# Four of eight row-tile pairs by seven products in the gate and up projections of a hybrid layer

## The chip, the cores and the metric

The kernel runs on one core of one Trainium2 chip. The metric is the device time of one execution in microseconds (us). Before the change it is 1145.84 us, the median of three runs (1144.41 to 1147.18).

## The reference

One decoder layer for 256 tokens of width 2048, all in float32: a low-rank attention with 8 heads beside a state-space mixer, an output projection with a residual, a gated feed-forward part, and a gated embedding at the end. The change touches the feed-forward part, whose hidden width is 5632:

```python
x = x + mixed @ w_o[i]
hf = rms_norm(x, g_ffn_norm[i])
x = x + (jax.nn.silu(hf @ w_gate[i]) * (hf @ w_up[i])) @ w_down[i]
gate = jax.nn.sigmoid(rms_norm(x, g_ple_norm[i]) @ w_ple_gate[i])
x = x + gate * (p[i] @ w_ple_proj[i])
```

## The kernel before

**Products.** Every large matmul keeps float32 accuracy by splitting each operand into a rounded part and a remainder, hi and lo. One product of a 128 x 128 piece of activations with a 128 x 512 piece of weights is then three matmuls: hi*hi, hi*lo, lo*hi (`products`, all recorded under line L359).

**Weights.** They come in chunks of 256 rows by 512 columns (512 KB, tile `w_raw`, five buffers, loaded by the SyncE queue SP at L169). ScalarE (ACT) rounds a chunk into `w_hi` (L195), VectorE (DVE) subtracts to get `w_lo` (L196); of each there are three buffers. `split_to` and `load_to` run ahead of the matmuls by these buffers.

**Gate and up.** Eleven blocks of 512 hidden columns. In each, eight pairs j = 0..7: the gate chunk and the up chunk of the same 256 rows. Each pair has two row tiles k, two halves t of the tokens, and two matrices: a 2 x 2 by 2 x 2 matrix product of pieces, eight products. For the pairs in `MIXED` (2, 4, 6; in the first block 4, 6) a scheme with seven products is used. It needs sums of weight pieces, made by `mix`: four additions (`w_sum`, L210), the hi of the up chunk's last piece and of the two sum tiles on ACT (L213), and the lo of the same on DVE (L214, `w_last` and `w_mix`). It also needs sums of the activations (`sum`, made once by `norm_task`). There is one set of `w_last`, `w_sum` and `w_mix`, so the sums of the next mixed pair can only be written when PE has read those of the last.

**End of a block.** The gate and up sums stand in four PSUM banks (`acc`), shared products of the mixed pairs in four others (`pp_p`). `shared` combines the latter after the last mixed pair; then for each half t: DVE adds `acc` to `wsg`, ACT applies Silu, DVE subtracts `uc` from `acc`, DVE multiplies (all L343). The next block's matmuls need those `acc` banks. `gate_task` transposes `wsg` into `g` (PE, `pp_g`).

**Order.** The code is written in a plain order, and a scheduler sets each engine's order from it by priorities: `split_to` and `mix` stand 70 places ahead (`W_AHEAD`), `AHEAD` lists other tasks. Each engine runs its own list strictly in that order, and SP does too.

**Memory.** 39 slots of 4 KB per partition (`Slots`) hold all larger tiles. The residual rows `xs` (four slots) are made before the gate and up stage, lie through it, and are next used after the first block of the down projection.

Of the kernel before, what the change touches and what calls it, by code (L numbers as in the profile page):

```python
# [81 lines left out]


W_AHEAD = 70

AHEAD = {'s5_params': -50, 'x_stats': 50, 'glu_out': -25, 'gate_task': -25, 'norm_task': -100, 'latent_norms': -50, 'z_task': -200, 'head_norms': -200}

# [54 lines left out]
class Weights:  # L142
# [4 lines left out]
    def __init__(self, tc, pool, sched):  # L147
        self.tc, nc = tc, tc.nc
        self.nc, self.pool, self.sched, self.chunks = nc, pool, sched, []
        self.raw, self.part, self.n_dma, self.n_split = {}, {}, 0, 0  # L150
        self.extra, self.native = {}, set()
        self.mixed, self.kept, self.sums = set(), {}, None

    def block(self, w, k0, nk, c0, n):
        ids = []
# [9 lines left out]
    def load_to(self, i):  # L165
        while self.n_dma <= min(i, len(self.chunks) - 1):
            w, k, c0, n = self.chunks[self.n_dma]
            t = self.pool.tile([128, 2, n], F32, tag="raw", bufs=self.RAW, name="w_raw")
            self.nc.sync.dma_start(  # L169
                out=t, in_=w[k * 128:(k + 2) * 128, c0:c0 + n].rearrange("(k p) n -> p k n", p=128)  # L170
            )
            self.raw[self.n_dma] = t
            self.n_dma += 1
            for out, in_ in self.extra.pop(self.n_dma, ()):
                self.nc.sync.dma_start(out=out, in_=in_)

    def split_to(self, i):
        while self.n_split <= min(i, len(self.chunks) - 1):
# [14 lines left out]
            lo = self.pool.tile([128, 2, n], F32R, tag="w_lo", bufs=self.PART, name="w_lo")  # L193
            with self.tc.high_priority(W_AHEAD):
                self.nc.scalar.activation(out=hi, in_=raw, func=AF.Copy)  # L195
# [7 lines left out]
    def mix(self, g, u):  # L203


        V, A, s = self.nc.vector, self.nc.scalar, self.sched
        last, raws, parts = self.sums

        def add(o, a, b):
            V.tensor_tensor(out=o, in0=a, in1=b, op=ALU.add)  # L210

        def part(h, l, r):
            A.activation(out=h, in_=r, func=AF.Copy)  # L213
            V.tensor_tensor(out=l, in0=r, in1=h.bitcast(F32), op=ALU.subtract)  # L214

        with self.tc.high_priority(W_AHEAD):
            add(raws[0][:, 0], g[:, 0], u[:, 0])
            add(raws[0][:, 1], u[:, 0], u[:, 1])
            part(last[:, 0], last[:, 1], u[:, 1])
            add(raws[1][:, 0], raws[0][:, 0], u[:, 1])  # L220
            add(raws[1][:, 1], raws[1][:, 0], g[:, 1])
            for r, (h, l) in zip(raws, parts):
                part(h, l, r)
        s.act += 5 * 512 * 0.83e-3 + 3 * 0.19
        s.dve = max(s.dve + 9 * 512 * 1.05e-3 + 0.42, s.act)
        (h0, l0), (h1, l1) = parts
        return ((last[:, 0], last[:, 1]), (h0[:, 0], l0[:, 0]), (h0[:, 1], l0[:, 1]),
                (h1[:, 0], l1[:, 0]), (h1[:, 1], l1[:, 1])), None, s.dve

    def take(self, i):  # L230
        self.split_to(i + self.PART - 1)
        self.load_to(i + self.PART - 1 + self.RAW)
        hi, lo, t = self.part.pop(i)
        self.sched.pe = max(self.sched.pe, t)
        return hi, lo
# [3 lines left out]
def hybrid_layer_kernel(  # L239
# [6 lines left out]
    nc = tc.nc  # L246
# [7 lines left out]
    dram = ctx.enter_context(tc.tile_pool(name="scratch", bufs=1, space=bass.MemoryType.DRAM))  # L254

    S = Slots(big, [f"s{i}" for i in range(39)])
    PP = Slots(psb, [f"pp{i}" for i in range(4)])
    sched = Sched(tc)
    W = Weights(tc, wts, sched)

    blk = {}
# [13 lines left out]
    blk["glu"] = [W.block(w_glu, 0, 8, 512 * b, 512) for b in range(2)]  # L275
    blk["wos"] = [W.block(w_o, 8, 8, 512 * b, 512) for b in range(4)]
    blk["gu"] = []
    MIXED = (2, 4, 6)
    for b in range(11):
        ids = []  # L280
        for j in range(8):
# [8 lines left out]
    def wait_get(shape, name, dtype=F32):  # L290
        n = 0
        while True:
            t = S.try_get(shape, name, dtype)
            if t is not None:
                return t
            sched.step()
            sched.pe += 1.0
            n += 1
            if n > 2000:
                raise RuntimeError(f"no slot for {name}: {S.held()}")  # L300

    def wait_n(n, shape, name, dtype=F32):
        return [wait_get(shape, name, dtype) for _ in range(n)]
# [18 lines left out]
    r_a, r_s, r_f, r_p = (stat(n, 2) for n in ("r_a", "r_s", "r_f", "r_p"))  # L322
# [19 lines left out]
    def tt(o, a, b, op=ALU.mult):  # L342
        V.tensor_tensor(out=o, in0=a, in1=b, op=op)  # L343
        sched.dve += size(o) * 1.05e-3 + 0.1
# [9 lines left out]
    def act(o, i, f, **k):  # L354
        A.activation(out=o, in_=i, func=f, **k)  # L355
        sched.act += size(o) * 0.83e-3 + 0.19 + 0.09 * sum(n in k for n in ("accum_out",))
# [86 lines left out]
    NWU = 30  # L443
    X0, B0, NE = 18, 8, 22
    GATE = "y0"


    def s5_params():
# [778 lines left out]
    acc = block(blk["zq"], lhs_h, need_h)  # L1227
# [3 lines left out]
    acc = block(blk["zkv"], lhs_h)  # L1231
# [6 lines left out]
    acc = block(blk["u"][0], lhs_h)  # L1238
# [3 lines left out]
    acc = block(blk["u"][1], lhs_h)  # L1242
# [26 lines left out]
    xs = [wait_n(2, [128, 1024], "xs") for _ in range(2)]  # L1269
# [13 lines left out]
    for p, (lo, hi) in enumerate(blk["woa"]):  # L1283
        acc = accs2(), accs2()
# [74 lines left out]
    fh = wait_n(4, [128, 4, 256], "fh", F32R)  # L1359
    fl = wait_n(4, [128, 4, 256], "fl", F32R)  # L1360
    rows = {j: wait_get([128, 2, 512], "sum", F32R) for j in MIXED}
    lhs_s = tiles4(sh, sl, 8)
# [4 lines left out]
    for b in range(4):  # L1367
        acc = block(blk["wos"][b], lhs_s, need_s)
# [6 lines left out]
    lhs_f = tiles4(fh, fl)  # L1375
    wsg = wait_n(2, [128, 2, 512], "wsg")
    uc = wait_get([128, 2, 512], "uc")
    W.sums = (wait_get([128, 2, 512], "w_last", F32R), wait_n(2, [128, 2, 512], "w_sum"),
              [wait_n(2, [128, 2, 512], "w_mix", F32R) for _ in range(2)])
    gr, gh, gl = [], [], []  # L1380

    def gate_task(b):
# [92 lines left out]
    for b in range(11):  # L1475
        ws = wsg[b % 2]
        acc = mixed_block(blk["gu"][b], lhs_f, rows, ws, uc, need_f)
        if b == 0:
            total_rstd(r_f, ss_f)
        for t in range(2):  # L1480
            tt(ws[:, t], ws[:, t], acc[2 * t], ALU.add)
            act(ws[:, t], ws[:, t], AF.Silu, scale=r_f[:, t:t + 1])
            tt(uc[:, t], acc[2 * t + 1], uc[:, t], ALU.subtract)
            tt(ws[:, t], ws[:, t], uc[:, t])
        sched.add(gate_task(b), 0)
    S.put(*fh, *fl, *rows.values(), uc, W.sums[0], *W.sums[1], *W.sums[2][0], *W.sums[2][1])
    lhs_g = tiles4(gh, gl)

    def need_g(k):
# [9 lines left out]
    for b in range(4):  # L1499
        ph.append(wait_get([128, 4, 256], "ph", F32R))  # L1500
        pl.append(wait_get([128, 4, 256], "pl", F32R))
        acc = block(blk["down"][b], lhs_g, need_g)
# [119 lines left out]
```

## Time and profile before

| what | value |
|---|---|
| runs before, median | 1145.84 us |
| the profiled execution | 1146.05 us, its span 1144.1 us |
| gate and up stage in the span | 317.5 to 796.4 us |
| down stage | 796.4 to 1039.5 us |
| granted TensorE clock | 0.998 |

Rows of groups read: line, engine, operation, output<-inputs, shapes, count | busy us, mean ns of one | idle time before them and what ended it. Rows of stretches read: start:end, length, then busy us (and number of instructions) of PE, PEld (weight loads), DVE, ACT, POOL, the granted clock, the DMA share and GB/s. Rows in order of time read: start, length, what.

### The profile page before, as it was taken

What the parts mean: (1) busy time and instruction counts of PE and PEld (TensorE: products, weight loads), DVE (VectorE), ACT (ScalarE), POOL (GpSimd) and SP (SyncE); (2) the same over time, 40 slices, a digit from 0 to 9 for tenths busy, and PEclk for the clock granted to TensorE, in tenths of its full rate; (3) what the DMA queues carried; (4) which work ended last, traced back from release to release, by engine and by line L of the source; (5) the groups of instructions that cost most, each with busy time, mean ns of one, the idle gap of its engine ahead of it and who ended that gap; (6) DMA issues with size and microseconds to landing.
All of it is one profiled execution on the core that took longest, in us unless ns stands there. A gap on an engine that the chain in (4) does not pass through costs nothing.

```text
span 1144.1 us, 15655 instructions
## 1 busy us (share of the span) xinstructions
PE 1117.7 (98%) x5842; PEld 923.7 (81%) x5842; DVE 861.4 (75%) x1233; ACT 648.3 (57%) x921; POOL 19.0 (2%) x40
## 2 busy tenths in 40 slices
PE   9998999999999999999999999999999999999998
PEld 6877877889887877877877877878888888888886
DVE  7988999658698898888898898899645454546554
ACT  7863994636665555655655655557534344436443
POOL 1000020000000000000000000000000000000000
PEclk9999999999999999999999999999999999999999
DMA  9996471355566656665665665665665655555662
GB/s 336 247 259 191 117 229 33 109 190 179 183 187 200 204 184 185 204 196 180 211 192 178 210 186 178 217 183 184 202 194 186 197 188 191 188 192 187 213 209 91
DMA packets 112188, 216.97 MB, mean 190 GB/s; under 512 B 8032, under 2 KB 12912, under 8 KB 112112
## 3 DMA queue, kind: packets, MB, share of 16 engines
q1 hardware_dynamic: 109808, 211.23, 58.9%
q0 software_dynamic: 2304, 4.74, 1.5%
q8 instruction: 46, 0.75, 0.3%
q14 instruction: 30, 0.25, 0.1%
HBM read 212.66 MB, written 3.28 MB: 189 GB/s over the span
## 4 chain that ended last, share of the span: by engine, by line
PE 78%; DVE 9%; DMA 5%; ACT 4%; issue 2%; POOL 0%; DVEq 0%; SPq 0%; ACTq 0%; POOLq 0%
PE acc L359 67%; PE pp_p L359 5%; DMA w_raw<-in_w_up_dram 4%; DVE w_lo L196 3%; ACT w_hi L195 2%; DMA e<-in_bE_dram 1%; PE pp_g L386 1%; PE pp_at L359 1%; DVE w L750 1%; PE pp_at L1003 1%; PE pp_n L386 1%; PE pp_v L731 1%; DVE w_sum L210 1%; ACT L355 1%; PE pp_y L785 1%
## 5 line engine op out<-in xcount | busy, mean ns | idle before, releaser
L196 DVE TENSOR_TENSOR w_lo<-w_raw,w_hi 128x1024 fp32r<-128x1024 f32 (+2 forms) x350 | 420.8, 1206 | 207.4 <-ACT w_hi L195 206.1
L195 ACT ACTIVATE w_hi<-w_raw 128x1024 fp32r<-128x1024 f32 (+2 forms) x350 | 366.1, 1047 | 350.7 <-PE acc L359 318.9
L359 PE MATMUL acc<-w_hi,fh 128*128 128x512 f32 x480 | 188.7, 396 | 5.9 <-DVE uc L343 5.8
L359 PE MATMUL acc<-w_lo,fh 128*128 128x512 f32 x480 | 188.1, 392 | 0.0
L359 PE MATMUL acc<-w_hi,fl 128*128 128x512 f32 x480 | 187.1, 390 | 0.0
L359 PE MATMUL acc<-w_hi,gh 128*128 128x512 f32 x352 | 137.3, 390 | 0.0
L359 PE MATMUL acc<-w_hi,gl 128*128 128x512 f32 x352 | 137.1, 389 | 0.0
L359 PE MATMUL acc<-w_lo,gh 128*128 128x512 f32 x352 | 137.0, 389 | 0.0
L359 PEld LDWEIGHTS acc<-w_hi,fh 128*128 128x128 f32 x480 | 90.1, 188 | 30.9 <-DVE uc L343 12.4
L359 PEld LDWEIGHTS acc<-w_hi,fl 128*128 128x128 f32 x480 | 90.1, 188 | 18.8
L359 PEld LDWEIGHTS acc<-w_lo,fh 128*128 128x128 f32 x480 | 90.2, 188 | 17.5 <-DVE w_lo L196 0.2
L213 ACT ACTIVATE w_mix<-w_sum 128x1024 fp32r<-128x1024 f32 x64 | 67.9, 1062 | 50.3 <-DVE w_sum L210 38.5
L359 PEld LDWEIGHTS acc<-w_hi,gl 128*128 128x128 f32 x352 | 66.1, 188 | 13.8
L359 PEld LDWEIGHTS acc<-w_lo,gh 128*128 128x128 f32 x352 | 66.1, 188 | 13.6
L359 PEld LDWEIGHTS acc<-w_hi,gh 128*128 128x128 f32 x352 | 66.1, 188 | 13.6 <-DVE uc L343 0.2
L214 DVE TENSOR_TENSOR w_mix<-w_sum,w_mix 128x1024 fp32r<-128x1024 f32 x64 | 76.3, 1218 | 0.6
L359 PE MATMUL pp_p<-w_mix,sum 128*128 128x512 f32 x288 | 70.5, 389 | 0.0
L359 PEld LDWEIGHTS pp_p<-w_mix,sum 128*128 128x128 f32 x288 | 54.1, 188 | 11.2
L210 DVE TENSOR_TENSOR w_sum<-w_raw 128x512 f32<-128x512 f32 x64 | 42.2, 687 | 27.7 <-DMA w_raw<-in_w_up_dram 26.5
L359 PE MATMUL acc<-w_hi,ph 128*128 128x512 f32 x128 | 49.8, 389 | 0.0
L359 PE MATMUL acc<-w_lo,ph 128*128 128x512 f32 x128 | 49.8, 389 | 0.0
L359 PE MATMUL acc<-w_hi,pl 128*128 128x512 f32 x128 | 49.8, 389 | 0.0
(308 smaller groups left out, 1713.0 us busy)
## 6 DMA issues: line engine op xcount, KB each, us to landing
w_raw<-in_w_gate_dram SPq DMA_DIRECT2D x88, 512.0 KB, 4.2
w_raw<-in_w_up_dram SPq DMA_DIRECT2D x88, 512.0 KB, 4.6
w_raw<-in_w_down_dram SPq DMA_DIRECT2D x88, 512.0 KB, 3.7
w_raw<-in_w_o_dram SPq DMA_DIRECT2D x32, 512.0 KB, 3.7
w_raw<-in_w_ple_gate_dram SPq DMA_DIRECT2D x32, 512.0 KB, 4.1
w_raw<-in_w_in_dram SPq DMA_DIRECT2D x24, 512.0 KB, 7.6
w_raw<-in_w_glu_dram SPq DMA_DIRECT2D x8, 512.0 KB, 4.4
w_raw<-in_w_uq_dram SPq DMA_DIRECT2D x8, 384.0 KB, 3.5
```

Of the source, the lines that this page charges most:

```text
L195: self.nc.scalar.activation(out=hi, in_=raw, func=AF.Copy)
L196: self.nc.vector.tensor_tensor(out=lo, in0=raw, in1=hi.bitcast(F32), op=ALU.subtract)
L210: V.tensor_tensor(out=o, in0=a, in1=b, op=ALU.add)
L213: A.activation(out=h, in_=r, func=AF.Copy)
L214: V.tensor_tensor(out=l, in0=r, in1=h.bitcast(F32), op=ALU.subtract)
L355: A.activation(out=o, in_=i, func=f, **k)
L359: T.matmul(out=o, lhsT=a, rhs=b, start=start, stop=stop)
L386: T.transpose(out=o, in_=i, identity=ident if idt is None else idt)
L731: T.matmul(out=pv[p, r * 256 + i4 * 64:r * 256 + i4 * 64 + 64], lhsT=ee[r][p, i * 64:i * 64 + 64], rhs=um[p, i, :], start=True, stop=True, ...
L750: V.tensor_tensor_scan(out=w, data0=dc, data1=w, initial=0.0, op0=ALU.mult, op1=ALU.add)
L785: T.matmul(out=o, lhsT=a[p, i, :], rhs=f[p, i, :], start=False, stop=(r == 1), tile_position=(64 * s, 64 * s))
L1003: T.matmul(out=o, lhsT=a, rhs=b_, start=False, stop=(i == 1), skip_group_check=True)
```

## The change

Four pairs of each block are mixed, (2, 3, 5, 6), in the first block (3, 5, 6). There are two sets of `w_last` and `w_mix`, used in turn; `w_sum` stays single. Two more weight buffers (`w_more`) take the chunks whose number modulo 7 is 0 or 3, so seven chunks can lie in SBUF. The slots for this come from `xs`, whose four tiles are copied to DRAM (`x_keep`) by the POOL queue and copied back after the stage. The instructions of a block's end are written with a priority of 100 places and in another order: both additions to `wsg`, then both subtractions, then both products.

```diff
@@ class Weights
-            t = self.pool.tile([128, 2, n], F32, tag="raw", bufs=self.RAW, name="w_raw")
+            if self.more and self.n_dma % 7 in (0, 3) and self.n_dma < self.more_end:
+                self.more.rotate(1)
+                t = self.more[0]
+            else:
+                t = self.pool.tile([128, 2, n], F32, tag="raw", bufs=self.RAW, name="w_raw")
...
-        last, raws, parts = self.sums
+        last, raws, parts = self.sums[0]
+        self.sums.rotate(1)
...
     def take(self, i):
-        self.split_to(i + self.PART - 1)
-        self.load_to(i + self.PART - 1 + self.RAW)
+        n, j = 0, i
+        while n < self.PART and j < len(self.chunks):
+            n += j not in self.mixed
+            j += 1
+        if j in self.mixed:
+            j += 1
+        self.split_to(j - 1)
+        self.load_to(j - 1 + self.RAW + len(self.more))
...
-    MIXED = (2, 4, 6)
+    MIXED = (2, 3, 5, 6)
...
+    NSET = 2
...
+    w_sum = wait_n(2, [128, 2, 512], "w_sum")
+    for _ in range(NSET):
+        W.sums.append((wait_get([128, 2, 512], "w_last", F32R), w_sum,
+                       [wait_n(2, [128, 2, 512], "w_mix", F32R) for _ in range(2)]))
+    W.more_end = blk["down"][0][0]
+    W.more.extend(wait_n(2, [128, 2, 512], "w_more"))
...
-        for t in range(2):
-            tt(ws[:, t], ws[:, t], acc[2 * t], ALU.add)
-            act(ws[:, t], ws[:, t], AF.Silu, scale=r_f[:, t:t + 1])
-            tt(uc[:, t], acc[2 * t + 1], uc[:, t], ALU.subtract)
-            tt(ws[:, t], ws[:, t], uc[:, t])
+        with tc.high_priority(G_AHEAD):
+            for t in range(2):
+                tt(ws[:, t], ws[:, t], acc[2 * t], ALU.add)
+                act(ws[:, t], ws[:, t], AF.Silu, scale=r_f[:, t:t + 1])
+            for t in range(2):
+                tt(uc[:, t], acc[2 * t + 1], uc[:, t], ALU.subtract)
+            for t in range(2):
+                tt(ws[:, t], ws[:, t], uc[:, t])
         sched.add(gate_task(b), 0)
+        if b == 2:
+            keep = [dram.tile([128, 1024], F32, name="x_keep") for _ in range(4)]
+            for i in range(4):
+                nc.gpsimd.dma_start(out=keep[i], in_=xs[i // 2][i % 2])
+                S.put(xs[i // 2][i % 2])
...
+    for i in range(4):
+        xs[i // 2][i % 2] = t = wait_get([128, 1024], "xs")
+        nc.gpsimd.dma_start(out=t, in_=keep[i])
```

The first place is DVE's list at the end of a block, from the last weight work before it on. Before, in the sixth block (L196 splits, L210 weight sums, L343 the block's end):

```order
L196 TENSOR_TENSOR w_lo<-w_raw,w_hi 128x1024 x3
L343 TENSOR_TENSOR uc<-wsg,pp_p 128x512
L343 TENSOR_TENSOR wsg<-uc,pp_p 128x512
L343 TENSOR_TENSOR uc<-uc 128x512
L343 TENSOR_TENSOR wsg<-wsg,acc 128x512
L343 TENSOR_TENSOR uc<-wsg,uc 128x512
L210 TENSOR_TENSOR w_sum<-w_raw 128x512 x2
L196 TENSOR_TENSOR w_lo<-w_raw,w_hi 128x1024
L343 TENSOR_TENSOR uc<-acc,uc 128x512
L343 TENSOR_TENSOR wsg<-wsg,acc 128x512
L343 TENSOR_TENSOR wsg<-wsg,uc 128x512
L196 TENSOR_TENSOR w_lo<-w_raw,w_hi 128x1024
```

And after, at the end of the fifth block (L201, L216, L220 and L355 are the former L196, L210, L214 and L343):

```order
L220 TENSOR_TENSOR w_mix<-w_sum,w_mix 128x1024
L201 TENSOR_TENSOR w_lo<-w_more,w_hi 128x1024
L216 TENSOR_TENSOR w_sum<-w_more,w_raw 128x512
L355 TENSOR_TENSOR uc<-wsg,pp_p 128x512
L216 TENSOR_TENSOR w_sum<-w_raw 128x512
L355 TENSOR_TENSOR wsg<-uc,pp_p 128x512
L220 TENSOR_TENSOR w_last<-w_raw,w_last 128x512
L355 TENSOR_TENSOR wsg<-wsg,acc 128x512
L355 TENSOR_TENSOR uc<-uc 128x512
L216 TENSOR_TENSOR w_sum<-w_sum,w_raw 128x512
L355 TENSOR_TENSOR uc<-wsg,uc 128x512
L355 TENSOR_TENSOR uc<-acc,uc 128x512
```

The first sum of the next block's pair 2 has moved ahead of all ten instructions of the block's end; the sums of that pair that followed each other now stand between them. The four instructions that free `acc` banks, which weight work parted before, stand closer together.

The second place is the SP list with buffer numbers, around the loads for pair 2 of the same block. Before, 5092 and 5119 are gate and up of pair 2, and 5017, 5038, 5062 and 5080 the chunks of pairs 0 and 1:

```order
L169 DMA w_raw_5017<-in_w_gate_dram 128x2x512
L169 DMA w_raw_5038<-in_w_up_dram 128x2x512
L169 DMA w_raw_5062<-in_w_gate_dram 128x2x512
L169 DMA w_raw_5080<-in_w_up_dram 128x2x512
L169 DMA w_raw_5092<-in_w_gate_dram 128x2x512
L169 DMA w_raw_5119<-in_w_up_dram 128x2x512
```

After, pair 2 is w_more_3490 (gate) and 5080 (up), and 3489, 5016, 5018 and 5061 are pairs 0 and 1:

```order
L174 DMA w_more_3489<-in_w_gate_dram 128x2x512
L174 DMA w_raw_5016<-in_w_up_dram 128x2x512
L174 DMA w_raw_5018<-in_w_gate_dram 128x2x512
L174 DMA w_more_3490<-in_w_gate_dram 128x2x512
L174 DMA w_raw_5061<-in_w_up_dram 128x2x512
L174 DMA w_raw_5080<-in_w_up_dram 128x2x512
```

The order is almost that of the chunks, with some loads one place early. A load waits for the buffer of the chunk that came seven chunks earlier instead of five: the up chunk of pair 2 for the gate chunk of pair 7 of the block before, where it waited for the gate chunk of pair 0 of its own block.

The POOL list gains eight entries after the loads of `xs`: four `x_keep<-xs`, four `xs<-x_keep`, and behind them the load of `pr` that was there before.

More of the change, by code (lines that the diff above doesn't have):

```diff
@@ L84 @@
 W_AHEAD = 70
+G_AHEAD = 100
 AHEAD = {'s5_params': -50, 'x_stats': 50, 'glu_out': -25, 'gate_task': -25, 'norm_task': -100, 'latent_norms': -50, 'z_task': -200, 'head_norms': -200}
@@ L151, in __init__ @@
         self.extra, self.native = {}, set()
-        self.mixed, self.kept, self.sums = set(), {}, None
+        self.mixed, self.kept, self.sums, self.more = set(), {}, deque(), deque()
     def block(self, w, k0, nk, c0, n):
@@ L1377, in hybrid_layer_kernel @@
     uc = wait_get([128, 2, 512], "uc")
-    W.sums = (wait_get([128, 2, 512], "w_last", F32R), wait_n(2, [128, 2, 512], "w_sum"),
-              [wait_n(2, [128, 2, 512], "w_mix", F32R) for _ in range(2)])
+    w_sum = wait_n(2, [128, 2, 512], "w_sum")
[4 more added lines that the diff above has]
+    W.more.extend(wait_n(2, [128, 2, 512], "w_more"))
     gr, gh, gl = [], [], []
@@ L1479, in hybrid_layer_kernel @@
             total_rstd(r_f, ss_f)
-        for t in range(2):
-            tt(ws[:, t], ws[:, t], acc[2 * t], ALU.add)
-            act(ws[:, t], ws[:, t], AF.Silu, scale=r_f[:, t:t + 1])
-            tt(uc[:, t], acc[2 * t + 1], uc[:, t], ALU.subtract)
-            tt(ws[:, t], ws[:, t], uc[:, t])
-        sched.add(gate_task(b), 0)
-    S.put(*fh, *fl, *rows.values(), uc, W.sums[0], *W.sums[1], *W.sums[2][0], *W.sums[2][1])
+        with tc.high_priority(G_AHEAD):
[6 more added lines that the diff above has]
+                tt(ws[:, t], ws[:, t], uc[:, t])
+        sched.add(gate_task(b), 0)
+        if b == 2:
[3 more added lines that the diff above has]
+                S.put(xs[i // 2][i % 2])
+    more = list(W.more)
+    W.more.clear()
+    S.put(*more, *fh, *fl, *rows.values(), uc, *w_sum)
+    for last, _, parts in W.sums:
+        S.put(last, *parts[0], *parts[1])
+    for i in range(4):
+        xs[i // 2][i % 2] = t = wait_get([128, 1024], "xs")
+        nc.gpsimd.dma_start(out=t, in_=keep[i])
     lhs_g = tiles4(gh, gl)
```

## The prediction

> **What bounds the kernel now.** I read the page's shares first, then the chain that ended last.
>
> ```profile
> PE 1117.7 (98%) x5842; PEld 923.7 (81%) x5842; DVE 861.4 (75%) x1233; ACT 648.3 (57%) x921; POOL 19.0 (2%) x40
> PE 78%; DVE 9%; DMA 5%; ACT 4%; issue 2%; POOL 0%; DVEq 0%; SPq 0%; ACTq 0%; POOLq 0%
> ```
>
> PE is busy nearly all the time and carries 78% of the chain. DVE and DMA carry 14%, so PE is held up by them somewhere. Where, the stretches of the gate and up stage show: the whole stage, its first block, a middle block, and the last.
>
> ```profile
> 317.50:796.40 478.90, 472.22 (x2106) 385.41 (x2105) 419.57 (x507) 282.15 (x323) 0.00 (x0) 1.00 0.63 194
> 317.70:361.80 44.10, 43.99 (x199) 36.15 (x197) 38.76 (x65) 28.59 (x38) 0.00 (x0) 1.00 0.64 192
> 580.30:623.80 43.50, 42.89 (x192) 35.00 (x192) 37.69 (x45) 24.80 (x29) 0.00 (x0) 1.00 0.63 194
> 754.60:796.60 42.00, 42.00 (x188) 34.58 (x189) 40.62 (x46) 28.03 (x33) 0.00 (x0) 1.00 0.63 201
> ```
>
> A middle block takes 43.5 us; the last, with the same matmuls and no block behind it, 42.0 with PE never idle. So 1.5 us a block is lost at the boundary between blocks. DVE works 37.7 of 43.5 us: 87% here, against 75% over the kernel. The stage, and not the average, decides what four more DVE microseconds a block do. Next the chain through one boundary, merged, and PE's own rows there:
>
> ```profile
> 614.85 1.24 DVE w_lo L196
> 616.08 0.02 issue
> 616.10 4.56 DMA w_raw<-in_w_up_dram
> 620.66 0.02 issue
> 620.68 0.04 DVE w_sum L210
> ...
> 623.11 0.61 DVE uc L343
> 623.73 0.04 issue
> 623.77 2.34 PE acc L359 x9
> ```
>
> ```profile
> 621.41 0.39 PE L359 MATMUL acc<-w_hi,fl 128*128 128x512 f32 x1
> 622.77 0.39 PE L359 MATMUL acc<-w_hi,fl 128*128 128x512 f32 x1
> 623.77 0.50 PE L359 MATMUL acc<-w_hi,fh 128*128 128x512 f32 x1 [0.61 <-DVE uc L343]
> ```
>
> Between the first two rows stand six matmul intervals: (622.77 - 621.41) / 6 = 0.2267 us a matmul. Then 1.00 us passes: DVE freed the `acc` bank late, because weight sums stood ahead of that subtraction in its list and waited for a load. The load was issued when a split released its buffer, and took 4.56 us.
>
> **Seven products.** One more mixed pair saves one product, three matmuls, in each of 11 blocks: 33 x 0.2267 = 7.5 us, or 0.68 a block. All of it is on the path if PE is fed. The added pair adds no transpose.
>
> **DVE pays for it.** Here are DVE's rows of the block end, then two groups.
>
> ```profile
> 606.95 0.68 DVE L214 TENSOR_TENSOR w_last<-w_raw,w_last 128x512 fp32r<-128x512 f32 x1
> 607.55 2.35 DVE L214 TENSOR_TENSOR w_mix<-w_sum,w_mix 128x1024 fp32r<-128x1024 f32 x2
> 620.68 1.29 DVE L210 TENSOR_TENSOR w_sum<-w_raw 128x512 f32<-128x512 f32 x2 [0.53 <-DMA w_raw<-in_w_up_dram]
> 621.90 1.22 DVE L196 TENSOR_TENSOR w_lo<-w_raw,w_hi 128x1024 fp32r<-128x1024 f32 x1
> 623.03 0.68 DVE L343 TENSOR_TENSOR uc<-acc,uc 128x512 f32<-128x512 f32 x1
> 623.63 0.68 DVE L343 TENSOR_TENSOR wsg<-wsg,acc 128x512 f32<-128x512 f32 x1
> ```
>
> ```profile
> L210 DVE TENSOR_TENSOR w_sum<-w_sum,w_raw 128x512 f32<-128x512 f32 x64 | 43.8, 684 | 0.3
> L213 ACT ACTIVATE w_mix<-w_sum 128x1024 fp32r<-128x1024 f32 x64 | 67.9, 1062 | 50.3 <-DVE w_sum L210 38.5
> ```
>
> A recorded 0.68 us lets the next instruction start after 0.60 (623.03 to 623.63), a recorded 1.22 after 1.13 (621.90 to 623.03). A mixed pair adds four sums and one `w_last` at 0.60 and two `w_mix` at 1.13, and drops one `w_lo` at 1.13: 5 x 0.60 + 1.13 = 4.13 us a block. On the recorded 37.7 that makes 41.8. Counted anew by starts, twelve splits, four mixes of 5.27 and ten block-end instructions are 12 x 1.13 + 4 x 5.27 + 10 x 0.60 = 40.6. The difference is the tail of each instruction that has nothing ready behind it; the new list puts independent work between dependent pairs, so the truth lies between.
>
> PE fed would take 42.0 - 0.68 = 41.3 a block. Both engines are then full, and what DVE still waits for decides. The waits of the same block before:
>
> ```profile
> ACT w_hi L195 <- PE acc L359: 8.1, 7, 1.7
> DVE w_lo L196 <- ACT w_hi L195: 2.5, 3, 1.4
> DVE w_sum L210 <- DMA w_raw<-in_w_up_dram: 2.3, 2, 1.8
> ```
>
> The 2.5 us for ACT is back-pressure: ACT waits for PE to leave a `w_hi` buffer, so DVE was ahead. It goes when DVE has no lead. The 2.3 us for loads is not. With seven buffers one load stays late: the up chunk of pair 2, whose buffer is released by the gate split of pair 7. Between that split and the first sum of pair 2 the list holds a split, a `w_mix` and a split, 3 x 1.13 = 3.4 us, while issue and load take 0.02 + 4.56 = 4.6. DVE pauses 1.2 us, ahead of the block's end; behind it are the ten instructions that free the banks and the first up split, which PE needs after 12 matmuls (2.7 us) of the next block. By the list, all other loads have over 7 us of DVE work between release and use. So a middle block takes 40.6 + 1.2 = 41.8 to 41.8 + 1.2 = 43.0 us. I take 42.5, nearer the upper end: a split that starts after ACT has no way to hide its tail.
>
> **Boundary.** What is freed first is now in the order in which PE asks for it, and 11 instructions from the first to the last subtraction last 11 x 0.60 = 6.6 us, against 5.4 us (24 matmuls) of the last pair plus the 0.68 until the second bank is needed. The 1.5 us lost there become at most some 0.5, included in the 42.5.
>
> **ACT.** It gains two `w_mix` at 1.06 and a `w_last` of half the size, and loses one `w_hi` of the size of a `w_mix`: under 2.1 us a block on 24.8, hidden. It also runs in order: its `w_last` of pair 3 stands ahead of Silu, and would hold it until that load lands, some 3 us after the last pair begins; the multiplication that needs Silu stands over 6 us after. No cost.
>
> **First block.** 44.1 us, with DVE at 38.8 and rows of the residual in it; with 4.1 more and the pause, DVE has 44.1, and one more row sum (four additions of 0.28 us and one of 0.68) lies there or just before. I take 44.7.
>
> **Last block.** No block follows, so DVE does not bind: 41.3 + 0.3 = 41.6.
>
> ```profile
> L343 DVE TENSOR_TENSOR rows<-rows x12: 280/284/293, 304.0 to 334.0; 128x128 f32<-128x128 f32 x12
> xs<-in_x_dram POOLq DMA_DIRECT2D x4, 512.0 KB, 6.9
> L351 DVE SCALAR_TENSOR_TENSOR xs<-acc,r_f,xs x8: 740/743/746, 857.2 to 1040.1; 128x512 f32<-128x512 f32 x8
> 796.40:1039.50 243.10, 243.10 (x1090) 201.43 (x1089) 127.03 (x121) 107.33 (x120) 0.55 (x1) 1.00 0.59 191
> ```
>
> **Residual rows through DRAM.** Eight transfers of 512 KB on the POOL queue. The nearest row took 6.9 us. Four run early in the stage, as soon as `xs` is final, with DMA 0.64 busy; four at its end. Bounds: nothing, if they fill idle DMA time; or one late load, 4.6 us, each time. I take 0.7 in all, near nothing, since the rows come back some 60 us before their use (the first such addition stood at 857.2, the stage's end at 796.4), `pr` behind them is needed later still, and weight loads run seven chunks ahead.
>
> **Splits of `g`.** Part of the DVE work for the down stage was done in the last gate block (40.62 against 37.69 busy); now more moves behind it. DVE is busy 127 of 243 us there: hidden.
>
> **Sum.** 44.7 + 9 x 42.5 + 41.6 = 468.8 against 478.9: -10.1, and 0.7 back: -9.4. The profiled execution took 1146.05 us (span 1144.1, so 1.95 around it), 0.02% over the median of 1145.84. 1146.05 - 9.4 = 1136.6. A change under 0.2% (2.3 us) can't be told from none.
>
> **A rule against it.** The rows make DVE the fuller engine of the stage: 419.57 of 478.9, 88%, with weight loads on PE at 385.41, 80%. The Trainium skill, "Perfetto Trace Analysis", section "Identifying the Most-Contended Engine", says to judge TensorE by weight-load busy share instead of matmul busy time, and to relieve the engine with the highest occupancy first. By that rule this change relieves the wrong engine: the saved 7.5 us would give nothing and the added DVE time would decide, which is the third rival below with its 1164, against 1136.6 by the rows. The trace agrees on which engine is fuller; that PE, idle-free in the last block, needs 42.0 there shows that PE binds all the same.
>
> **Rivals.** *PE fully fed.* If nothing of DVE's waits remains, the stage is 43.4 + 10 x 41.3 = 456.4: -22.5, so 1123.6, with DVE's 40.6 as support. Against it speaks the 1.2 us pause: 40.6 + 1.2 is over 41.3. Chance 0.13, mostly its upper half, 1124 to 1131.
>
> *No change.* If no instruction of the added mix overlaps the next, because each waits for ACT, the recorded lengths count: 5 x 0.68 + 1.22 = 4.62, so 37.7 + 4.6 + 1.2 = 43.5 a block, as before: 44.7 + 9 x 43.5 + 41.6 = 477.8, with the 0.7 about 1145.7. The sums, which stand `x2` at 1.29 together, speak against it. Chance 0.14. The Trainium skill, "VectorE: DVE Perf Modes", section "The TRN2 errata", gives (N + 151) / 0.96 ns for such an addition, 691 at N = 512, and 1224 by estimate at 1024; with these the added pair costs 4.68 and the sum is 1146. The trace agrees with them as recorded lengths (0.68, 1.22), not as spacing.
>
> *Slower: DVE binds with its old pauses.* A middle block has 43.5 - 37.7 = 5.8 us of DVE idle. Where more than 43.5 - 41.8 = 1.7 stays, each block is longer than before. If the 2.3 for loads stays, and one 1.4 wait of a split for ACT, because ACT stands in its own list behind a load or a buffer, a block is 41.8 + 3.7 = 45.5 and the stage 17 us longer: 1164. Chance 0.16; an idle of 2.2 a block, just over the tipping point, would end at 1150.
>
> **How the numbers follow.** Likeliest, with 0.57: 1136.6, its own range 1131 to 1143 (41.8 to 43.2 a block). Faster by over 0.2%: this case and the fed one, with a little of the rest, 0.71; within: 0.13; slower: 0.16. The range, 1126 to 1148, holds all but the slower case and the lowest part of the fed one.
>
> **What would show it.** DVE busy 41 to 42 us in a block of the stage, PE busy some 41.5 to 42, blocks of 42 to 43. One wait of DVE for an up chunk of 1 to 1.5 us a block, and PE's wait for `uc` or `wsg` at boundaries under 0.5, perhaps a wait for `w_lo` in its place. I am wrong if DVE's idle time per block stays over 1.7 us, if ACT blocks on `w_last`, or if PE is fed and blocks fall under 41.8.

## The result, and the profile after

| | before | after |
|---|---|---|
| median of the runs | 1145.84 us (1144.41 to 1147.18) | 1138.17 us (1134.82 to 1140.22) |
| ratio, 95% interval | | 0.9929 [0.9905, 0.9954] |
| profiled execution, span | 1146.05, 1144.1 us | 1135.29, 1133.2 us |

The change made the kernel 0.7% faster; 1136.6 us had been forecast. By the medians it saved 7.7 us, by the two profiled executions 10.8; the profiled execution of the changed kernel was one of its faster ones. The shares of busy time and of the chain that ended last, from the page of the changed kernel (a name that ends in q is that engine's sequencer):

```profile
PE 1112.5 (98%) x5809; PEld 919.6 (81%) x5809; DVE 899.2 (79%) x1304; ACT 664.6 (59%) x946; POOL 23.3 (2%) x48
PE 56%; DVE 28%; issue 6%; DMA 5%; ACT 3%; DVEq 0%; POOL 0%; SPq 0%; ACTq 0%; POOLq 0%
```

PE has 33 matmuls fewer (5842 to 5809) and DVE works 38 us more. PE's share of the chain fell from 78% to 56%, DVE's rose from 9% to 28%: DVE now stands on over a quarter of the chain. Whether DVE's speed is what sets a block's length is another question, which e4 answers. Stretches of the gate and up stage, first of before (its nine middle blocks), then of after (first block, nine middle blocks, last block):

```profile
361.80:754.60 392.80, 386.23 (x1720) 314.70 (x1720) 340.20 (x398) 225.34 (x255) 0.00 (x0) 1.00 0.62 193
```

```profile
315.70:362.60 46.90, 44.85 (x195) 36.77 (x194) 43.16 (x66) 28.42 (x39) 1.58 (x3) 0.96 0.67 217
362.60:743.10 380.50, 379.56 (x1693) 309.68 (x1692) 367.93 (x458) 237.68 (x272) 0.00 (x0) 1.00 0.64 199
743.10:785.20 42.10, 42.00 (x188) 34.18 (x187) 41.87 (x49) 33.25 (x38) 2.66 (x5) 1.00 0.71 231
```

A middle block went from 392.80 / 9 = 43.6 to 380.50 / 9 = 42.3 us. DVE is busy 367.93 / 9 = 40.9 us of it. The first block got longer, 44.1 to 46.9. The stage took 469.5 us against 478.9, 9.3 us less: the nine middle blocks gained 12.3, and the first gave 2.8 of it back. The rest of the 10.9 us between the two spans is not the change's: the stage began at 315.7 instead of 317.8 us, and this point lay anywhere from 315.5 to 322.8 us in the profiles of this study. Behind the stage 0.5 us was lost.

The boundary whose pause of 1.00 us the prediction showed, in the changed kernel, DVE's rows and then PE's:

```profile
616.01 0.68 DVE L355 TENSOR_TENSOR uc<-acc,uc 128x512 f32<-128x512 f32 x1
616.61 0.68 DVE L355 TENSOR_TENSOR wsg<-wsg,acc 128x512 f32<-128x512 f32 x1
617.20 0.69 DVE L355 TENSOR_TENSOR uc<-acc,uc 128x512 f32<-128x512 f32 x1
617.80 0.68 DVE L355 TENSOR_TENSOR wsg<-wsg,uc 128x512 f32<-128x512 f32 x1
618.40 1.22 DVE L201 TENSOR_TENSOR w_lo<-w_raw,w_hi 128x1024 fp32r<-128x1024 f32 x1
```

```profile
616.75 0.50 PE L371 MATMUL acc<-w_hi,fh 128*128 128x512 f32 x1
...
619.06 0.48 PE L371 MATMUL acc<-w_hi,fh 128*128 128x512 f32 x1
619.67 0.50 PE L371 MATMUL acc<-w_lo,fh 128*128 128x512 f32 x1
```

PE starts the next block as soon as the bank is free, and what it waits for now is the first `w_lo` of the up matrix: 619.67 - 619.06 = 0.61 us between two matmuls instead of 0.23, since the split at 618.40 stands behind the block's end. The waits of DVE for loads and ACT, and of PE for DVE, over eight blocks (405 to 740 us) are all small; columns are total, times, longest:

```profile
DVE w_lo L201 <- ACT w_hi L200: 5.2, 8, 0.9
DVE w_sum L216 <- DMA w_raw<-in_w_up_dram: 4.7, 6, 1.0
PEld acc L371 <- DVE w_lo L201: 3.1, 8, 0.5
PEld acc L371 <- DVE uc L355: 1.5, 4, 0.5
DVE w_sum L216 <- DMA w_more<-in_w_up_dram: 1.1, 2, 0.6
```

### The profile page after: what moved, and what is told of

It is laid out like the page before. It is cut to its first block, busy times and chain, and to the rows that moved or that the text cites. A ratio compares the mean times of both kernels' runs of the same rounds, so it can differ in the third digit from the quotient of the medians.

```text
span 1133.2 us, 15659 instructions
## 1 busy us (share of the span) xinstructions
PE 1112.5 (98%) x5809; PEld 919.6 (81%) x5809; DVE 899.2 (79%) x1304; ACT 664.6 (59%) x946; POOL 23.3 (2%) x48
## 4 chain that ended last, share of the span: by engine, by line
PE 56%; DVE 28%; issue 6%; DMA 5%; ACT 3%; DVEq 0%; POOL 0%; SPq 0%; ACTq 0%; POOLq 0%
PE acc L371 48%; DVE w_lo L201 9%; DVE w_sum L216 7%; DMA w_raw<-in_w_up_dram 3%; DVE w_mix L220 3%; PE pp_p L371 3%; DVE uc L355 2%; DVE w_last L220 2%; DVE wsg L355 1%; DMA e<-in_bE_dram 1%; PE pp_at L371 1%; DVE w L763 1%; ACT w_hi L200 1%; PE pp_at L1016 1%; PE pp_v L744 1%
## 5 line engine op out<-in xcount | busy, mean ns | idle before, releaser
L201 DVE TENSOR_TENSOR w_lo<-w_raw,w_hi 128x1024 fp32r<-128x1024 f32 (+2 forms) x302 | 362.6, 1205 | 185.7 <-ACT w_hi L200 185.2
L200 ACT ACTIVATE w_hi<-w_raw 128x1024 fp32r<-128x1024 f32 (+2 forms) x302 | 314.6, 1044 | 291.1 <-PE acc L371 257.9
L371 PE MATMUL acc<-w_hi,fh 128*128 128x512 f32 x403 | 159.7, 396 | 0.1
L371 PE MATMUL acc<-w_lo,fh 128*128 128x512 f32 x403 | 158.3, 393 | 0.8
L371 PE MATMUL acc<-w_hi,fl 128*128 128x512 f32 x403 | 157.4, 391 | 0.0
L219 ACT ACTIVATE w_mix<-w_sum 128x1024 fp32r<-128x1024 f32 x86 | 91.0, 1058 | 70.5 <-DVE w_sum L216 69.4
L220 DVE TENSOR_TENSOR w_mix<-w_sum,w_mix 128x1024 fp32r<-128x1024 f32 x86 | 104.8, 1219 | 0.3 <-ACT w_mix L219 0.2
L371 PE MATMUL pp_p<-w_mix,sum 128*128 128x512 f32 x387 | 95.3, 390 | 2.0 <-DVE fl L363 2.0
L371 PEld LDWEIGHTS acc<-w_hi,fl 128*128 128x128 f32 x403 | 75.9, 188 | 15.7
L371 PEld LDWEIGHTS pp_p<-w_mix,sum 128*128 128x128 f32 x387 | 72.4, 188 | 17.9 <-issue 2.4
L200 ACT ACTIVATE w_hi<-w_more 128x1024 fp32r<-128x1024 f32 x37 | 39.0, 1054 | 14.5 <-PE acc L371 5.7
```

The source lines that it names most:

```text
L201: self.nc.vector.tensor_tensor(out=lo, in0=raw, in1=hi.bitcast(F32), op=ALU.subtract)
L371: T.matmul(out=o, lhsT=a, rhs=b, start=start, stop=stop)
```

## The experiments

Every experiment was timed against the kernel before on the same chip. Below stand its median and ratio, and from its trace: the first part of the stage (from its first matmul to the last product of the first block into a `pp_p` bank), the mean block (from there to the same point of the eleventh block, divided by ten), the whole stage, and what lies behind it.

| kernel | time us | ratio, 95% | first part | mean block | stage | behind |
|---|---|---|---|---|---|---|
| before | | 1 | 36.74 | 43.58 | 478.86 | 347.44 |
| after | 1138.17 | 0.9929 [0.9905, 0.9954] | 39.97 | 42.32 | 469.53 | 347.95 |
| e1: block's end alone | 1140.94 | 0.9950 [0.9934, 0.9966] | 36.74 | 43.07 | 473.76 | 348.65 |
| e2: three pairs | 1141.73 | 0.9953 [0.9937, 0.9968] | 37.96 | 42.64 | 470.70 | 348.88 |
| e4: less DVE work | 1136.48 | 0.9908 [0.9889, 0.9928] | 37.53 | 42.35 | 467.40 | 348.40 |
| e5: stores on SP | 1139.26 | 0.9933 [0.9912, 0.9953] | 36.69 | 42.70 | 470.09 | 347.53 |
| e7: eight buffers | 1141.05 | 0.9946 [0.9927, 0.9964] | 38.14 | 42.14 | 467.01 | 354.47 |
| e8: eight, less DVE work | 1136.44 | 0.9914 [0.9889, 0.9940] | 37.99 | 41.88 | 464.24 | 352.60 |
| e3: five buffers | 1142.22 | 0.9958 [0.9942, 0.9974] | 41.07 | 42.68 | 474.22 | 348.25 |
| e6: old block's end | 1169.00 | 1.0192 [1.0169, 1.0214] | 39.81 | 45.03 | 496.50 | 348.93 |
| e10: eight, splits of g first | 1136.19 | 0.9895 [0.9881, 0.9909] | 37.55 | 42.13 | 465.18 | 348.58 |
| e11: e10, stores on SP | 1133.51 | 0.9875 [0.9861, 0.9888] | 36.69 | 42.18 | 464.85 | 348.47 |
| e12: e11, three pairs | 1143.77 | 0.9979 [0.9967, 0.9991] | 36.74 | 43.17 | 474.83 | 347.36 |

**e1, the order of the block's end alone.** The kernel before, with nothing but this:

```diff
+        with tc.high_priority(G_AHEAD):
             for t in range(2):
                 tt(ws[:, t], ws[:, t], acc[2 * t], ALU.add)
                 act(ws[:, t], ws[:, t], AF.Silu, scale=r_f[:, t:t + 1])
+            for t in range(2):
                 tt(uc[:, t], acc[2 * t + 1], uc[:, t], ALU.subtract)
+            for t in range(2):
                 tt(ws[:, t], ws[:, t], uc[:, t])
```

> The kernel before, with one part of the change: the instructions of a block's end in the new order and with the priority of 100 places. Three mixed pairs, five weight buffers, one set of sums, residual rows in SBUF. My theory: a middle block before takes 43.55 us, of which about 1.5 are lost because DVE frees the accumulator banks late; the new order takes away 0.4 to 1.0 of it, so a block of 42.6 to 43.1 and 1136 to 1142 us. Rival: the order alone does nothing, because the weight sum that waits for its load still stands ahead of the block's end; a block of 43.4 to 43.7 and 1144 to 1147.

The block fell by 0.51 us and the stage by 5.1: over half of the change's gain in the stage, with no product saved and no buffer added.

**e2, three mixed pairs in the changed kernel.**

```diff
-    MIXED = (2, 3, 5, 6)
+    MIXED = (2, 4, 6)
```

> The changed kernel with three mixed pairs (2, 4, 6; in the first block 4, 6) instead of four; all the rest of the change stays. My theory: DVE, busy 40.6 to 41.0 of 42.2 to 42.4 us a block, binds the changed kernel; without the fourth pair it has 36.5 to 37 and PE is never held up, so a block of 42.0 to 42.3 with PE busy throughout, against 42.4, and 1133 to 1139 us in all: the fourth pair gave nothing. Rival: PE still binds with four pairs and the saved product is the gain, so a block of 43.0 to 43.2 and 1143 to 1146.

Neither range held: the block of 42.64 lies between the two, and so does the time. Against e1 the second set, the two buffers and the residual rows in DRAM took 3.1 us off the stage; the fourth pair, from e2 to the changed kernel, 1.2. In the blocks it gives 0.32 us of the 0.68 that three matmuls are worth, and in the first block it takes 2.0 us back. Most blocks of e2 last 42.40 to 42.45 us, and PE waits there for almost nothing: with three pairs PE was already fed. The 7.5 us that the fourth pair frees on PE thus arrive as 1.2 in these two profiles; the medians of e2 and of the changed kernel lie 3.6 us apart, with intervals that overlap.

**e4, less work for DVE.** The changed kernel; from the third mixed pair on, only 64 of 512 columns of the second sum tile's remainder are computed, some 3.7 us of DVE work a block less by count (the busy time fell by 323.98 - 297.67 = 26.3 us in 335, 3.3 a block):

```diff
-            for r, (h, l) in zip(raws, parts):
-                part(h, l, r)
+            for i, (r, (h, l)) in enumerate(zip(raws, parts)):
...
+                    V.tensor_tensor(out=l[:, :, 0:64], in0=r[:, :, 0:64], ...)
```

> The changed kernel, where from the third mixed pair on the remainder of the second sum tile is computed for 64 of 512 columns only, so that some 3.7 us of DVE work a block are left out and PE does the same. My theory: DVE binds, so a block falls from 42.4 to 41.5 to 41.8 (PE's 180 matmuls and eight transposes), 6 to 9 us less than the changed kernel: 1129 to 1133. Rival: DVE's load does not matter, and waits for loads or ACT hold PE; a block of 42.2 to 42.5 and 1136 to 1140.

The block did not move: 42.35 us. (The stage is 2.1 us shorter all the same, by its first block; e5 comes back to that.) The view of waits (405 to 740 us) and DVE's row at a boundary say why:

```profile
DVE w_sum L216 <- DMA w_raw<-in_w_up_dram: 17.8, 8, 3.3
DVE w_sum L216 <- DMA w_more<-in_w_up_dram: 5.8, 4, 2.3
```

```profile
396.50 1.29 DVE L216 TENSOR_TENSOR w_sum<-w_raw 128x512 f32<-128x512 f32 x2 [3.62 <-DMA w_raw<-in_w_up_dram]
397.71 0.68 DVE L220 TENSOR_TENSOR w_last<-w_raw,w_last 128x512 fp32r<-128x512 f32 x1
398.31 0.69 DVE L216 TENSOR_TENSOR w_sum<-w_sum,w_raw 128x512 f32<-128x512 f32 x1
398.91 1.22 DVE L201 TENSOR_TENSOR w_lo<-w_raw,w_hi 128x1024 fp32r<-128x1024 f32 x1
400.05 0.68 DVE L360 TENSOR_TENSOR uc<-wsg,pp_p 128x512 f32<-128x512 f32 x1
```

DVE's waits for up loads rose from 5.8 to 23.6 us in these eight blocks, 2.2 a block more. DVE reaches the first sum of pair 2 earlier and stands there until the load has landed, and the block's end (400.05) stands behind it in DVE's list. So DVE's throughput alone does not set the block. A second theory took its place: a loop through this load (release of its buffer, load, first sum, block's end, next release).

**e7 and e8, an eighth buffer, without and with the less of DVE work.**

```diff
-            if self.more and self.n_dma % 7 in (0, 3) and self.n_dma < self.more_end:
+            if self.more and self.n_dma % 8 in (0, 3, 5) and self.n_dma < self.more_end:
...
-    W.more.extend(wait_n(2, [128, 2, 512], "w_more"))
+    W.more.extend(wait_n(3, [128, 2, 512], "w_more"))
```

> The changed kernel with a third extra weight buffer (eight in all, chunks whose number modulo 8 is 0, 3 or 5 go to the extra ones): the up load of pair 2 is then released by the sums of pair 6, one split earlier than by the gate split of pair 7. Theory (a loop through that load sets the block: release, some 4.6 us of load, first weight sum, block end, banks): DVE's wait for the up load at the block's end falls from some 0.8 us a block to under 0.3, a middle block goes from 42.41 to 41.6-42.1, the time to 1130-1135. Rival (DVE's throughput sets the block at 42.4 with its small waits for ACT and PE): unchanged, 42.3-42.5 and 1137-1139. Third way: PE's own waits for the first up split and for a bank (about 1 us a block together) stay whatever DVE does: 42.2-42.5 with the wait for the load gone.

> Eight weight buffers and, as in e4_less_dve, of the remainder of the second sum tile only 64 of 512 columns from the third mixed pair on (some 3.7 us of DVE work a block left out). Theory (load loop and DVE throughput are two limits nearly equal): with both taken away PE is fed, a middle block falls to 41.3-41.6, the stage to some 460, the time to 1127-1130. Rival (the load loop alone binds): the same as e7_eight_bufs within 0.2 us a block. Third way (something on PE's own side, neither loads nor DVE time): 42.2-42.5 as in e4_less_dve.

Stretches of 405 to 740 us, for after, e4, e7 and e8, one row each in this order (length, PE, PE weight loads, DVE, ACT, POOL, clock, DMA share, GB/s):

```profile
405.00:740.00 335.00, 334.16 (x1490) 272.87 (x1490) 323.98 (x395) 207.18 (x237) 0.00 (x0) 1.00 0.65 201
```

```profile
405.00:740.00 335.00, 333.58 (x1490) 273.81 (x1491) 297.67 (x397) 204.62 (x237) 0.00 (x0) 1.00 0.64 200
```

```profile
405.00:740.00 335.00, 334.68 (x1498) 274.14 (x1497) 328.83 (x400) 207.52 (x240) 0.00 (x0) 1.00 0.66 201
```

```profile
405.00:740.00 335.00, 334.94 (x1506) 276.19 (x1505) 305.36 (x401) 213.18 (x241) 0.00 (x0) 1.00 0.65 201
```

Less DVE work alone changes the block by +0.03 us, the eighth buffer alone by -0.18, both together by -0.44. In e7 DVE is busy 328.83 of 335 us, 98%: there it is full. In e8 it is at 91%, PE waits for DVE under 0.3 us a block, and most blocks last 41.8 us. That is what PE itself needs: 180 matmuls of 0.2267 are 40.8, the transposes and the changes between banks the last us. So three limits lie within one microsecond: PE at 41.8, DVE at some 41.4 busy with little slack, and the load loop at 42.35. Two details missed. The wait for up loads did not fall under 0.3 us a block in e7 (4.0 us in eight blocks against 5.8). What fell with the eighth buffer is PE's wait for `w_lo`, from 3.1 to 0.3 us, so it may have helped by giving splits a lead rather than by removing that wait; no run separates the two. And e7 as a whole was no faster, as 6.5 us were lost behind the stage (e10).

**e9, pairs 3, 4, 5 and 6.** With three mixed pairs in a row the code writes the third sums into the first set before the products of the first are issued; this kernel computes something else, and its time says nothing on the load loop.

> The changed kernel with pairs 3, 4, 5, 6 mixed (first block 4, 5, 6): the first weight sum of a block now needs the up load of pair 3, whose buffer is released by the gate split of pair 0 of the same block, six splits (some 6.8 us) ahead of it. Theory (load loop): the wait for the up load at the block's end goes; but four sum groups stand in a row, each 6.4 us of DVE work against 4.76 us of PE, so that DVE falls up to 6.6 us behind in the middle of a block with two sets to cover it; a middle block of 41.8-42.5. Rival (DVE throughput): the same total of DVE work, 42.4 or, by the clustering, 42.5-43.5.

It took 1173.11 us. Nothing follows.

**e3, five buffers.** The changed kernel without the line `W.more.extend(...)`.

> The changed kernel without the two extra weight buffers (five in all). Theory (loads released late make DVE wait ahead of the block's end): the load that the first weight sum needs is released two chunks later, about 2 x 2.6 us, so DVE waits some 3 to 5 us a block more and a middle block takes 44.5-46.5; stage some 20 to 40 us longer, 1157-1177. Rival (loads hidden, DVE throughput binds): 42.4-42.8 and 1138-1141.

The rival's figure was the better one: 0.36 us a block, not 2 to 4. DVE's wait for up loads rose only from 5.8 to 10.8 us in eight blocks. The two buffers are worth 4.7 us of the stage, 1.1 of them in the first block, where in e3 one reload of `xs` also ran, at 325.73, probably since slots were free. The load loop is a limit next to the others, not far above them.

**e6, the old block's end in the changed kernel.** The edit of e1 undone, all else kept.

> The changed kernel with the block's end as before the change (no priority of its own, each half finished before the next). Theory (the order was worth 0.47 us a block alone; with DVE nearly full, banks freed late cost at least as much): a middle block of 42.8-43.3 instead of 42.3-42.4, stage 5-9 us longer, 1142-1147, PE waiting for uc or wsg at each boundary for some 0.5-1 us. Rival (with two sets and seven buffers no weight sum waits there any more, and the order is worth nothing): 42.3-42.5 and 1137-1139.

27 us longer in the stage, slower than before the change by 1.9%: the direction was expected, the size was not. In ten blocks PE issues the first product with `w_mix` of the next block's pair 2 ahead of that block's other products; the table's first part and mean block leave these early products aside. DVE's rows at one boundary, the row of PE that waits, and the view of waits of the same eight blocks:

```profile
497.19 1.22 DVE L220 TENSOR_TENSOR w_mix<-w_sum,w_mix 128x1024 fp32r<-128x1024 f32 x1
498.32 0.69 DVE L355 TENSOR_TENSOR uc<-wsg,uc 128x512 f32<-128x512 f32 x1
498.93 1.22 DVE L201 TENSOR_TENSOR w_lo<-w_raw,w_hi 128x1024 fp32r<-128x1024 f32 x1
500.06 1.22 DVE L220 TENSOR_TENSOR w_mix<-w_sum,w_mix 128x1024 fp32r<-128x1024 f32 x1
501.20 1.22 DVE L201 TENSOR_TENSOR w_lo<-w_more,w_hi 128x1024 fp32r<-128x1024 f32 x1
502.33 0.68 DVE L355 TENSOR_TENSOR wsg<-wsg,acc 128x512 f32<-128x512 f32 x1
```

```profile
503.07 0.80 PE L371 MATMUL acc<-w_hi,fh 128*128 128x512 f32 x1 [3.88 <-DVE wsg L355]
```

```profile
PE acc L371 <- DVE wsg L355: 15.7, 7, 3.9
```

Without a priority of its own the addition that frees the first bank stands behind two splits and two `w_mix`, 4 x 1.13 = 4.5 us of weight work for later pairs, and PE stands still for 3.88 us of it. About 5 us of the 27 are a consequence of such waits: 33 matmuls of the stage start 0.43 us apart instead of 0.23, against 8 in the changed kernel (see the last section). In the kernel before, the same order cost 5 us; in the changed kernel, with some 3 us more of DVE's time busy in each block, it costs 27. That DVE's load makes the difference is the likely reason, but the two kernels differ in buffers and pairs too, and no run takes these apart. The block's end is therefore no side matter of this change: with it the change gains 0.7%, without it it loses 1.9%.

**e5, the stores of x_keep on the SP queue**, written in each of the first four blocks instead of four on POOL near the stage's start. SP's list has them earlier than that: the trace shows them at 296.64, 320.84 (two) and 328.57, so the last three go out over 7.7 us instead of 1.6, still within the first block.

```diff
-        if b == 2:
+        if b == 0:
             keep = [dram.tile([128, 1024], F32, name="x_keep") for _ in range(4)]
-            for i in range(4):
-                nc.gpsimd.dma_start(out=keep[i], in_=xs[i // 2][i % 2])
-                S.put(xs[i // 2][i % 2])
+        if b < 4:
+            nc.sync.dma_start(out=keep[b], in_=xs[b // 2][b % 2])
+            S.put(xs[b // 2][b % 2])
```

> The changed kernel, with the copies of the residual rows to DRAM issued by SP between the weight loads, one in each of the first four blocks, instead of three at once by POOL at the start of the stage. My theory: in the first block the three copies delay a load of pair 5 (7.5 us instead of 4.6), the row sum that PE needs there comes 2.2 us late, and after that gap PE's clock is halved for some 3.8 us; with the copies spread the first block falls from 46.9 to 43.5 to 45 us, and the time by 2 to 3.5 us, to 1134 to 1137. Rival: the late row sum is due to its place in DVE's list alone; the gap stays and the time is 1136 to 1140.

The first part fell by 3.3 us, back to that of the kernel before; the blocks after it took 0.4 us each more and gave it back, so the time did not fall. Why they did stays open. DVE's first sum of pair 5, first in e5, then in e4, where the stores are as in the changed kernel:

```profile
334.06 0.69 DVE L216 TENSOR_TENSOR w_sum<-w_more,w_raw 128x512 f32<-128x512 f32 x1
```

```profile
332.40 0.69 DVE L216 TENSOR_TENSOR w_sum<-w_more,w_raw 128x512 f32<-128x512 f32 x1 [0.79 <-DMA w_raw<-in_w_up_dram]
```

The changed kernel waited 1.66 us here. An up load near the stage's start took 6.0 us (median) there and 4.9 in e5 and before the change. With the stores as they were, e4 waited 0.79 us and its first part was 37.53, 0.8 over e5: so the stores cost 0.8 to 3.3 us in these profiles. The larger price includes a stretch of matmuls at half speed (last section), which e4 does not have. Whether it is the queue or the spacing of the stores that counts, e5 does not separate.

**e10 and e11, towards a better kernel.** e7 lost 6.5 us behind the stage. Its waits and a stretch there (785 to 880 us, and 786.0 to 797.5):

```profile
PEld acc L371 <- DVE gl L355: 1.5, 1, 1.5
PEld acc L371 <- DVE uc L355: 1.5, 1, 1.5
```

```profile
786.00:797.50 11.50, 8.28 (x26) 6.25 (x27) 10.61 (x13) 4.39 (x8) 0.00 (x0) 0.70 0.25 89
```

PE waits there for the last `uc` and the first `gl`, and runs a part of the stretch at half clock (0.70 over it). e10, on top of e7, writes the first splits of g ahead of the reload of `x_keep`, so that they get the free slots; e11 adds the edit of e5.

```diff
-    for i in range(4):
-        xs[i // 2][i % 2] = t = wait_get([128, 1024], "xs")
-        nc.gpsimd.dma_start(out=t, in_=keep[i])
...
+    need_g(0)
+    for i in range(4):
+        xs[i // 2][i % 2] = t = wait_get([128, 1024], "xs")
+        nc.gpsimd.dma_start(out=t, in_=keep[i])
```

> Eight buffers as in e7_eight_bufs, but the first four splits of g for the down stage are written ahead of the reload of x_keep, so that they get the free slots and the reload those of the weight buffers. Theory (e7_eight_bufs won 2.5 us in the stage and lost 6.5 us behind it because the third extra buffer took the free slot into which the first splits of g go): middle blocks 42.0-42.2 as there, what lies behind the stage back from 354.5 to 348-349.5, the time 1133-1136. Rival (the loss has another cause): 354 behind the stage, 1140-1142.

> e10_eight_first with the four stores of x_keep on the SP queue, one in each of the first four blocks, as in e5_keep_sp. Theory (the stores at the stage's start cost the first block some 2-3 us; in e5_keep_sp the later blocks gave it back because one late load is enough there to stop DVE, which an eighth buffer hides): first block 2-3 us shorter than in e10_eight_first, middle blocks 41.9-42.2, the time 1130-1134. Rival (a store in the queue of the loads costs as much as on a queue of its own): equal to e10_eight_first within 1 us.

In e10 what lies behind the stage came back to 348.6 us, as expected, and the stage kept its gain. Between e10 and e11 the first part differs by 0.9 us and the stage by 0.3: with eight buffers most of the stores' cost was already gone, and the rival of e11 was right for the stage. The medians lie 2.7 us apart, with intervals that overlap, and the start of the stage alone varies by more than that from profile to profile. e11 is the fastest kernel of the study: 1133.51 us, 0.9875 [0.9861, 0.9888], below the interval of the changed kernel.

**e12, three pairs in e11.**

> e11_eight_sp (eight buffers, stores on SP, first splits of g ahead of the reload) with three mixed pairs, 2, 4 and 6: 33 matmuls more. With seven buffers the fourth pair was worth 1.2 us of the stage (e2_three_pairs against the changed kernel), of 7.5 saved on PE. Theory (PE was already fed with three pairs, at 42.4 a block, and DVE's waits ate most of the fourth pair's gain; an eighth buffer removes part of these waits): three pairs gain nothing from the eighth buffer and stay at 42.4-42.5 a block, a stage of 466.5-468.5, so that the fourth pair is worth 2-4 us here, 1135-1138. Rival (the eighth buffer helps both alike): a stage near 466, 1-1.5 us over e11_eight_sp. If the fourth pair were worth its full 7.5, the stage would be 472.

Neither: a block of 43.17 us, longer than the 42.64 with seven buffers. From the chain of one block, and DVE's row there:

```profile
602.86 1.24 DVE w_lo L201
604.10 0.02 issue
604.11 4.69 DMA w_raw<-in_w_up_dram
```

```profile
608.83 0.69 DVE L216 TENSOR_TENSOR w_sum<-w_raw 128x512 f32<-128x512 f32 x1 [3.38 <-DMA w_raw<-in_w_up_dram]
```

Here it is an up chunk in the middle of a block that starts to load late, as the end of a split releases it, and DVE waits for it in each block, 24.1 / 8 = 3.0 us on average. One more buffer and one mixed pair less made a new late load. The run therefore does not price the fourth pair; why this load is late with eight buffers was not followed.

## Why the prediction came out right, step by step

- **The sum.** Stage 468.8 forecast, 469.5 measured; the kernel 1136.6 forecast, 1138.17 measured. That it came so near is partly luck, since errors cancel: the nine middle blocks took 380.5 us against 9 x 42.5 = 382.5, the last 42.1 against 41.6, the first 46.9 against 44.7. The shares of the gain were not as thought either: of the 9.3 us of the stage, e1 and e2 give 5.1 to the order of the block's end, 3.1 to sets and buffers, and 1.2 to the fourth pair, after which the change is named.
- **DVE pays 4.13 us a block.** 37.7 became 40.9 busy, near the count by starts (40.6) and under the recorded 37.7 with 4.13 added (41.8): the added pair cost 3.2 of busy time. The new list does put independent work between dependent pairs, and the rival "no change", which rested on no overlap, fell with it.
- **The pause for the up load of pair 2.** It was there, ahead of the block's end, (4.7 + 1.1) / 8 = 0.7 us a block instead of 1.2. e4 shows that it is a limit of its own: it grows when DVE gets faster. The wait of splits for ACT, which was to go, stayed with 5.2 / 8 = 0.65 us. Busy time and these two waits make up the block: 40.9 + 0.7 + 0.65 = 42.3.
- **Boundary.** PE's wait for `uc` fell to 1.5 / 8 = 0.2 us a block, and 3.1 / 8 = 0.4 for `w_lo` came in its place, as said. What the prediction did not see is how much hung on it: it credited the new order with 1.0 to 1.5 us of a boundary that existed before, while e6 shows that without it the changed kernel's stage is 27 us longer.
- **PE fed at 41.3.** Mis-sized by 0.5: e8, fed, needs 41.8. The 42.0 of the last block before was the wrong base: its row counts 188 matmuls and that of a middle block 192, of which one only starts at the window's end. PE ran the first product of that block, three matmuls, before the pause at the boundary, so ahead of 754.60. The 0.68 was thus taken off a stretch that lacked three matmuls already, and 0.68 of the 1.5 us put down to the boundary was not lost there. So the rival of 1123.6 was out of reach.
- **First block.** The term that was furthest off. It was put at 44.7; the rows say where 46.9 came from. First POOL's stores, then DVE's first sum, the last row sum, and PE:

```profile
317.09 1.58 POOL L1509 DMA_DIRECT2D x_keep<-xs  x3 [23.59 <-DVE rows L355]
```

```profile
331.68 0.69 DVE L216 TENSOR_TENSOR w_sum<-w_more,w_raw 128x512 f32<-128x512 f32 x1 [1.66 <-DMA w_raw<-in_w_up_dram]
...
341.64 0.68 DVE L355 TENSOR_TENSOR sum<-rows,sum 128x512 fp32r<-128x512 f32 x1
342.25 0.87 DVE L363 SCALAR_TENSOR_TENSOR fl<-pp_n,gc,fh 128x256 fp32r<-128x256 f32 x2
```

```profile
343.26 0.93 PE L371 MATMUL pp_p<-w_mix,sum 128*128 128x512 f32 x3 [2.04 <-DVE fl L363]
...
344.72 0.63 PE L371 MATMUL acc<-w_hi,fh 128*128 128x512 f32 x1
345.15 0.63 PE L371 MATMUL acc<-w_lo,fh 128*128 128x512 f32 x1
```

  Three stores of 512 KB go out within 1.6 us, a load behind them is late, DVE waits 1.66 us, the row sums move back, and PE waits 2.0 us for them. e5 confirms the cause: with the stores moved, DVE's wait is gone and the first part is 3.3 us shorter. About half of that is the stretch at half speed after PE's wait, which not every run with these stores has: e6 repeats it, with a first part of 39.81, and e4 does not. "0.7 in all, near nothing" was the wrong price for `x_keep`. The reloads at the stage's end were hidden, as said.
- **The slower rival.** It did not come about. e6, at 1169, is near its 1164 by accident: what holds PE in e6 is weight work ahead of the block's end (15.7 us of waits for `wsg` in eight blocks), and the change's own priority keeps that away. DVE's waits for up loads rose there too, from 5.8 to 12.4 + 4.6 = 17.0 us; whether as cause or consequence is not shown.
- **The rule of the fullest engine.** The Trainium skill, "Perfetto Trace Analysis", section "Identifying the Most-Contended Engine", would have relieved DVE first. The trace agrees that DVE is the fullest, 96.7% of 405 to 740 us (323.98 / 335) with PE's weight loads at 81% (272.87 / 335). The rule was right in that the 7.5 us saved on PE gave little, 1.2 in the stage. But the 1164 that went with it did not come, and relieving DVE alone did not help: e4 took 3.3 us a block of busy time from it and the block stayed at 42.35, because an in-order wait for a load took the freed time.

## What to carry to other kernels

Where an engine runs its list in order and is nearly full, put what frees another engine's buffers ahead of work for later, by priority: the order of the same ten instructions was worth 5 us in the kernel before, with DVE at 87%, and 27 us in the changed one, with DVE at 97%. When several limits lie within some 2% of each other (here PE 41.8, DVE 41.4, a load loop 42.35 us a block), relieving one moves little; take two away together before you call a theory dead. Transfers that the average load of the DMA engines would hide are not hidden where loads are already late, as at the start of this stage. And count the instructions of a stretch before taking it as a base: 188 and 192 matmuls are not the same block.

## What was not expected of the hardware

After PE's wait of 2.04 us at 343 the matmuls ran at half speed for a while: from 344.72 they start 0.43 us apart, (345.15 - 344.72), instead of 0.2267. The stretch around it, with the granted clock in the third column from the end:

```profile
343.30:347.20 3.90, 3.90 (x12) 3.17 (x13) 3.90 (x6) 1.97 (x2) 0.00 (x0) 0.68 0.00 1
```

Eight intervals at 0.2 us more each make some 1.6 us: nearly as dear as the wait itself. It does not follow every such wait: in e6 waits of 2.26 and 4.27 us between starts were followed by 7 and 11 slow matmuls, while others of 2.64, 2.79 and 2.88 us were followed by none. What decides it, no run here shows. The Trainium skill, "TensorE: Matmul & The Clock Gate", section "What's actually happening", has PE go to half clock after an idle window of about 3.4 us that runs freely. The spacing agrees with half a clock; the length does not, as 2.04 us of idle time sufficed here.
